# A hybrid attention layer on one core: three engines issue by one written list, values of four heads in one run

## The chip, the cores and the metric
The kernel runs on one NeuronCore of a Trainium2 chip. The core has five engines, each with its own instruction stream: TensorE (PE in the profile, its weight loads PEld), VectorE (DVE), ScalarE (ACT), GpSimd (POOL) and SyncE (SP), which here only issues DMAs. The metric is the device time of one execution in microseconds. Before the change the median of 3 runs is 233.36 us (233.3 to 233.59).

## The reference
One decoder layer for 256 tokens of 1024 channels, fp32, with two attention branches side by side:
```
mod = silu(c) @ w_ada + b_ada;  shift, scale, gate = split(mod, 3)
h = rms_norm(x, g_pre) * (1 + scale) + shift
proj = h @ w_in   # [q_lat 256 | kv_lat 128 | k_rope 32 | z_mla 512 | q,k,v,z_moba 4x512 | merge 2x1024]
# branch A: q = rms_norm(q_lat) @ w_uq, kv = rms_norm(kv_lat) @ w_ukv, rotary part of 32, one shared rotary key
# branch B: 8 heads of 64 with rotary q, k; for 256 tokens its block attention is a causal softmax
y_a = (softmax_A(q k) v * silu(z_mla)) @ w_o_mla;   y_b = (softmax_B(q k) v * silu(z_moba)) @ w_o_moba
y = (sigmoid(merge_a + b) * y_a + sigmoid(merge_b + b) * y_b) @ w_out
out = x + gate * rms_norm(y, g_post)
```

## The kernel before, in words
Precision first: nearly every matrix product of weights is made of three TensorE products of parts. A weight tile is split into a rounded part `w1` (ACT copies it into the type fp32r) and the rest `w2` (VectorE subtracts), and so are the activations (`h1`, `h2`); w1·h1, w1·h2 and w2·h1 are summed in one bank of PSUM. So every weight costs one ACT and one VectorE instruction per 512 columns (`split_one`, L251 to L280), which the profile shows under L266 or, where a helper records the order, under L82. PSUM has eight banks in four names of two each: `acc`, `sc`, `pv`, `tr`.

Weights come by DMA on SP's queue into five buffers `raw` of 8 KB a partition, in the order of `stream` (L200 to L206); `release` (L247) frees one when its last subtraction is issued and `pump` starts the next load. The split parts live in a ring of five tiles (`RING`).

The work has two stages. Up to about 62 us runs the projection of q, k, v of branch B over eight chunks of the contraction, with the modulation of each chunk computed just ahead; its order is written out in strings of tokens (`START`, `STEP`, `LAST`, L44 to L46; `s` is a split, `d` a subtraction, `P` a product, `V` the copy of the values) and kept on the engines by the helper `ordered` (L78). After that follow the latent projection of branch A (`lat_mm`, L516), the rotary embedding of branch B (`moba_rope`, `moba_tr`), 24 groups `F` (L431) that make the SiLU gates (kinds a and b) and the merge gates (kind g) from `win2`, the up-projections (`uq_*`, `ukv_*`), per head the scores and the softmax (`scores`, L656), the transposed probabilities (`p_tr`, L696) and the values of two heads (`pv`, L705), then the output products of both branches (`oproj`, L762), the gate row (`ada_gate`, L728) and the last product with w_out (`out_mm`, L887). A head's softmax is on VectorE mask and maximum (L684, L686), on ACT two exponentials (L689), on VectorE the reciprocal and two products (L690, L693).

In this second stage nothing is ordered by hand. The program issues the pieces in the sequence of L791 to L907, with F and the output products of branch B as fillers, and the framework's planner, which works with its own estimate of durations, places each engine's instructions; so an F may be broken by transposes, scores or values that become ready.

The values of a pair of heads are eight instructions, each head writing its 64 rows of one bank: two passes of 256 columns and two of 128 a head.

Of the kernel before, what the change touches and what calls it, by code (L numbers as in the profile page):

```python
# [18 lines left out]
P = 128  # L19
D = 1024  # L20
S = 256
H = 8
# [23 lines left out]
LAST = "P0v P1v P2v V P0q P0k P1q P2q P1k P2k"  # L46
POOL_LOW = []
# [15 lines left out]
def hybrid_layer_kernel(ctx: ExitStack, tc: tile.TileContext, x, head, cst, gpost, bgate,  # L63
# [128 lines left out]
    def ada_ab(j):  # L192
# [9 lines left out]
    stream += [(("f", 0), win2[0], 2048, 1), (("f", 1), win2[1], 2048, 1), (("uq",), wuq, 1536, 1),  # L202
               (("ukv",), wukv, 1024, 1)]
    stream += [(("f", i), win2[i], 2048, 1) for i in range(2, 12)]
# [17 lines left out]
    for key, src, n, parts in stream:  # L222
        if key[0] != "w":
            loads.append((key, src, 0, n))
        if key == ("out", 0, 0):
            order.append(("gate", 0))
            splits += [(("gate", 0), ("gate",), 0, a, a + 512) for a in (0, 512)]
# [6 lines left out]
        if key[0] == "f" and key[1] >= 8:  # L234
            loads.append((("g", key[1] - 8), wadag[key[1] - 8], 0, 2048))
    held, finished = [0], set()

    def pump():
        while loads and (loads[0] == "m" or held[0] < RAW or loads[0][0] in raws):
# [10 lines left out]

    def split_one():  # L251
        if not splits:
            return False
        u, key, c0, a, b = splits[0]
        if key not in raws or got.get(key, 2048) < c0 + b:
            return False
        if a == 0:
            i = order.index(u)
            if i >= RING and order[i - RING] not in finished:
                return False  # L260
            w1s[u] = rg.tile([P, 1024], FR, name="w1", bufs=RING)
            w2s[u] = rg.tile([P, 1024], FR, name="w2", bufs=RING)
        splits.pop(0)
        r = raws[key][:, c0 + a:c0 + b]
        w = key[0] == "w"
        free = lambda eng, f, *a, **k: f(*a, **k)  # L266
        o = ordered if w else free
        if u == ("w", 0, 0) and a == 0:
            o("V", V.tensor_copy, w1s[u][:, a:b], r)
        else:  # L270
            o("A", act, w1s[u][:, a:b], r, AF.Copy)
        rel = key != ("gate",) and (not splits or splits[0][1] != key)
        if w:
# [28 lines left out]
    def done_with(*us):  # L302
        finished.update(us)
        split_ahead()
# [9 lines left out]
    bR = bank("tr")  # L314

# [75 lines left out]
    def tokens(j, toks):  # L391
        for t in toks.split():
            if t == "s":
                if splits[0][1][0] == "w":
                    assert split_one(), splits[0]
            elif t == "d":
                if subs:
                    sub_one()
# [23 lines left out]
    assert splits[0][1][0] != "w" and not subs and len(vlast) == 2  # L422
    finished.update((("w", KT - 1, 0), ("w", KT - 1, 1)))
    split_ahead()
# [6 lines left out]
    def F():  # L431
        i = fcount[0]
        if i >= 24:
            return
# [9 lines left out]
        done_with(key)  # L444
        kind, m = ORDER[i]
        if kind == "g":
            act(tg[m // 8][:, m % 8], o, AF.Tanh, scale=0.5, bias=bmh[:, m:m + 1])
        else:
            th = wk.tile([P, S], FT, name="th", tag="hf", bufs=2)
            act(th, o, AF.Tanh, scale=0.5)  # L450
            z = wk.tile([P, S], FT, name="sz", bufs=5)
            V.scalar_tensor_tensor(z, th, 1.0, o, op0=OP.add, op1=OP.mult)
            sz[kind, m] = z
# [28 lines left out]
    def moba_tr(w, t):  # L482
        b = bank("tr")
        for i in range(4):
            nc.tensor.transpose(b[:, i * P:(i + 1) * P], rr[w][:, t, i * P:(i + 1) * P], ident)
        src = b.rearrange("p (k n) -> p k n", k=4)
# [15 lines left out]
    qlat = [sb.tile([P, 256], FT, name=f"qlat{t}") for t in range(2)]  # L502
    kvlat = [sb.tile([P, P], FT, name=f"kvlat{t}") for t in range(2)]
    kpe = sb.tile([P, 2, 32], FT, name="kpe")
    qpe = sb.tile([P, 2, 256], FT, name="qpe")
# [10 lines left out]
    def lat_mm():  # L516
        bA.extend(bank("tr") for _ in range(2))
        for i in range(4):
            key = ("l", i // 2, i % 2)
            w1, w2 = (w[:, :2 * NL].rearrange("p (k n) -> p k n", k=2) for w in weights(key))  # L520
            for k in range(2):
                for t in range(2):
                    kk = 2 * i + k
                    o, ha, hb = bA[t][:, :NL], h1[:, kk, t * P:(t + 1) * P], h2[:, kk, t * P:(t + 1) * P]
                    mm(o, ha, w1[:, k], start=(kk == 0), stop=False)
                    mm(o, hb, w1[:, k], start=False, stop=False)
                    mm(o, ha, w2[:, k], start=False, stop=(kk == KT - 1))
            done_with(key)
# [9 lines left out]

    def lat_evac():
        for t in range(2):  # L540
            rope_nat(bA[t][:, 384:416], t, 32, 2, kpe[:, t], V)
# [432 lines left out]
```

## Time and profile before
| | |
|---|---|
| median of 3 runs | 233.36 us |
| the profiled execution: time, span | 233.18 us, 231.4 us |
| TensorE busy, granted clock (mean) | 222.5 us (96%), 0.993 |
| VectorE busy | 169.4 us (73%) |
| ACT busy | 134.3 us (58%) |
| POOL busy | 50.8 us (22%) |
| longest wait of TensorE | 1.0 us |

How to read it: the span runs from the first to the last instruction of the profiled execution, and its time has some overhead around the span. Busy time counts overlapping instructions of one engine once. Matmuls are pipelined: their ends are modelled, so the distance from one start to the next says what one costs. An instruction of VectorE or ACT, too, is shown a little longer than the distance to the next one behind it.

### The profile page before, as it was taken

What the parts mean: (1) busy time and instruction counts of PE and PEld (TensorE: products, weight loads), DVE (VectorE), ACT (ScalarE), POOL (GpSimd) and SP (SyncE); (2) the same over time, 40 slices, a digit from 0 to 9 for tenths busy, and PEclk for the clock granted to TensorE, in tenths of its full rate; (3) what the DMA queues carried; (4) which work ended last, traced back from release to release, by engine and by line L of the source; (5) the groups of instructions that cost most, each with busy time, mean ns of one, the idle gap of its engine ahead of it and who ended that gap; (6) DMA issues with size and microseconds to landing.
All of it is one profiled execution on the core that took longest, in us unless ns stands there. A gap on an engine that the chain in (4) does not pass through costs nothing.

```text
span 231.4 us, 4325 instructions
## 1 busy us (share of the span) xinstructions
PE 222.5 (96%) x1578; PEld 191.6 (83%) x1578; DVE 169.4 (73%) x418; ACT 134.3 (58%) x320; POOL 50.8 (22%) x81
## 2 busy tenths in 40 slices
PE   8989999998999999999999999999999999999990
PEld 8846666665899999989879988989998799988890
DVE  1564554444999668989889998799996566899543
ACT  4364555554956668378775986348676534664320
POOL 2188888100045104300000000000400000562000
PEclk9999999999999999999999999999999999999997
DMA  6999998899855904432520536579799710000022
GB/s 249 348 412 406 378 318 307 274 302 331 314 200 181 353 27 170 129 144 74 187 106 13 173 96 244 208 270 302 290 372 416 292 61 0 1 3 0 0 91 91
DMA packets 10247, 47.05 MB, mean 203 GB/s; under 512 B 1137, under 2 KB 1649, under 8 KB 7154
## 3 DMA queue, kind: packets, MB, share of 16 engines
q1 hardware_dynamic: 10226, 46.78, 55.6%
q8 instruction: 12, 0.20, 0.3%
q14 instruction: 9, 0.07, 0.1%
HBM read 45.73 MB, written 1.05 MB: 202 GB/s over the span
## 4 chain that ended last, share of the span: by engine, by line
PE 91%; DVE 2%; issue 2%; ACT 2%; POOL 0%; POOLq 0%; DVEq 0%; ACTq 0%
PE acc L441 9%; PE acc L443 9%; PE acc L442 9%; PE pv L82 8%; PE sc L82 6%; PE acc L82 6%; PE tr L82 5%; PE pv L710 3%; PE acc L769 3%; PE tr L700 3%; PE acc L770 2%; PE acc L771 2%; PE sc L677 2%; PE sc L669 2%; PE sc L893 2%
## 5 line engine op out<-in xcount | busy, mean ns | idle before, releaser
L266 ACT ACTIVATE w<-raw 128x512 fp32r<-128x512 f32 (+1 forms) x93 | 52.3, 617 | 35.7 <-PE acc L442 9.6
L266 DVE TENSOR_TENSOR w<-raw,w 128x512 fp32r<-128x512 f32 (+1 forms) x93 | 63.8, 726 | 6.8 <-ACT w L266 5.8
L441 PE MATMUL acc<-h,w 128*128 128x256 f32 x184 | 53.1, 289 | 0.1
L443 PE MATMUL acc<-h,w 128*128 128x256 f32 x184 | 52.8, 287 | 0.0
L442 PE MATMUL acc<-h,w 128*128 128x256 f32 x184 | 52.3, 284 | 0.0
L441 PEld LDWEIGHTS acc<-h,w 128*128 128x128 f32 x184 | 34.7, 188 | 1.2 <-issue 0.7
L443 PEld LDWEIGHTS acc<-h,w 128*128 128x128 f32 x184 | 34.7, 188 | 0.6
L442 PEld LDWEIGHTS acc<-h,w 128*128 128x128 f32 x184 | 34.7, 188 | 0.3
L82 DVE TENSOR_TENSOR w<-raw,w 128x512 fp32r<-128x512 f32 x24 | 17.1, 732 | 14.0 <-ACT w L82 13.3
L741 POOL TENSOR_TENSOR gacc<-gacc,bgt 1x1024 f32<-1x1024 f32 x1 | 2.6, 2555 | 68.8 <-DMA raw<-in_wo_dram 68.8
L82 PE MATMUL sc<-w,h 128*128 128x512 f32 x48 | 16.6, 426 | 0.8 <-ACT xnT L82 0.5
L82 PE MATMUL pv<-w,h 128*128 128x512 f32 x48 | 15.5, 407 | 1.0 <-ACT w L82 1.0
L781 POOL TENSOR_TENSOR y<-yy,y 128x256 fp32r<-128x256 f32 x8 | 8.5, 1071 | 36.4 <-ACT y L780 36.4
L82 PE MATMUL acc<-w,h 128*128 128x512 f32 x48 | 15.6, 410 | 0.2 <-ACT h L82 0.2
L82 ACT ACTIVATE w<-raw 128x512 fp32r<-128x512 f32 x23 | 13.7, 619 | 1.6 <-DMA raw<-in_win_dram 1.6
L689 ACT ACTIVATE p<-p,mx 128x128 f32<-128x128 f32 (+1 forms) x32 | 14.2, 447 | 0.3 <-DVE mx L686 0.2
L82 PEld LDWEIGHTS sc<-w,h 128*128 128x128 f32 x48 | 8.0, 189 | 5.2 <-issue 2.9
L82 PEld LDWEIGHTS acc<-w,h 128*128 128x128 f32 x48 | 8.5, 188 | 4.3 <-ACT h L82 2.8
L82 PEld LDWEIGHTS pv<-w,h 128*128 128x128 f32 x48 | 8.5, 188 | 4.3 <-ACT w L82 3.0
L467 POOL TENSOR_TENSOR rr<-rr,m 128x512 f32<-128x512 f32 x4 | 5.6, 1420 | 25.6 <-DVE m L466 25.6
L693 DVE TENSOR_SCALAR p<-p,sm 128x128 f32<-128x128 f32 (+1 forms) x32 | 10.8, 380 | 0.1
L82 ACT ACTIVATE h<-xnT,ab 128x256 fp32r<-128x256 f32 x8 | 4.8, 601 | 10.3 <-DVE ab L82 8.8
(255 smaller groups left out, 525.9 us busy)
## 6 DMA issues: line engine op xcount, KB each, us to landing
raw<-in_win_dram SPq DMA_DIRECT2D x12, 1024.0 KB, 5.0
raw<-in_wada_dram SPq DMA_DIRECT2D x16, 512.0 KB, 7.2
raw<-in_win_dram SPq DMA_DIRECT2D x8, 512.0 KB, 7.6
raw<-in_wadag_dram SPq DMA_DIRECT2D x4, 1024.0 KB, 5.2
raw<-in_wo_dram SPq DMA_DIRECT2D x4, 1024.0 KB, 5.0
raw<-in_wout_dram SPq DMA_DIRECT2D x4, 1024.0 KB, 10.2
raw<-in_win_dram SPq DMA_DIRECT2D x8, 256.0 KB, 7.8
raw<-in_winl_dram SPq DMA_DIRECT2D x2, 832.0 KB, 6.9
```

The costliest lines, as they stand in the source:

```text
L82: r = f(*a, **k)
L266: free = lambda eng, f, *a, **k: f(*a, **k)
L441: mm(o, w1[:, k], h1[:, k], start=(k == 0), stop=False)
L442: mm(o, w1[:, k], h2[:, k], start=False, stop=False)
L443: mm(o, w2[:, k], h1[:, k], start=False, stop=(k == KT - 1))
L467: eng.tensor_tensor(dst, dst, m2, op=OP.add)
L689: act(p[:, a:e], p[:, a:e], AF.Exp, scale=scale, bias=mx[:, t:t + 1], accum_out=sm[:, t:t + 1])
L693: V.tensor_scalar(p[:, a:e], p[:, a:e], sm[:, t:t + 1], None, op0=OP.mult)
L700: nc.tensor.transpose(b[:, i * P:(i + 1) * P], p[:, i * P:(i + 1) * P], ident)
L710: mm(b[64 * i:64 * i + 64, 0:S], v[0][:, h * 64:h * 64 + 64], pTt[br, h][:, 0:S], start=True, stop=False, skip_group_check=True)
L769: mm(o, w1[:, k, c0:c0 + P], u1[br][:, k], start=(k == 0), stop=False)
L781: G.tensor_tensor(y2[:, m], yy, y1[:, m], op=OP.subtract)
```

## The change
TensorE, ACT and VectorE get their instructions in program order (`manual_schedule` for the three), from the first stage to the end; POOL and SP stay with the planner. The second stage is written as a list `PLAN` of 29 lines. A function that yields is a piece in two or three steps: its first token issues TensorE's part, its second (and third) the work on ACT and VectorE. `F` starts a gate group and `f` finishes the oldest one; `sb4` is the scores of heads 4 and 5 of branch b, its second call masks, maxima and exponentials, its third the normalising; `sa3` is one head of branch a; `tb4`, `ta3` transpose, `vb1`, `va0` are values of four heads; `s` and `d` are split and subtraction of the next weight piece, now of 1024 columns (832 for the latent projection); `A`/`y` and `B`/`b` start and finish output products; `G` is one gate sum; `O` the last product. The rest of the edits: values of four heads use one bank and one run; the products with the SiLU gate take 512 columns; loads are held to three from the end of the first stage to the last scores; the rotary key is copied to the other heads by three DMAs instead of two POOL copies and one of VectorE; four small query copies go from VectorE to ACT; the gate bias is added by VectorE.
```diff
-LAST = "P0v P1v P2v V P0q P0k P1q P2q P1k P2k"
+LAST = "s d P0v P1v P2v V s d s d P0q P0k P1q P2q P1k P2k"
...
-            cut = size // 2
-            splits += [(key + (i,), key, c0, a, e) for a, e in ((0, min(cut, m)), (cut, m)) if a < m]
+            cut = 512 if key[0] == "w" else m
+            splits += [(key + (i,), key, c0, a, min(a + cut, m)) for a in range(0, m, cut)]
...
+    in_order = tc.manual_schedule(engines={mybir.EngineType.PE, mybir.EngineType.Activation, mybir.EngineType.DVE})
+    in_order.__enter__()
...
+    cap[0] = RAW - 2
...
-        for x, n, e in ((a0[:, 1], P, "G"), (ak1, S, "V"), (aop["k2"], S, "G")):
-            dict(V=V, G=G)[e].tensor_copy(x[pe, 1:H], x[pe, 0:1].to_broadcast([32, H - 1, n]))
+        for x, n in ((ak1, S), (aop["k2"], S), (a0[:, 1], P)):
+            x = x.bitcast(FT)
+            nc.sync.dma_start(x[pe, 1:H], x[pe, 0:1].to_broadcast([32, H - 1, n]))
...
+    def pv(br, g):
         v = va if br == "a" else vb
         b = bank("pv")
-        for i in range(2):
-            h = 2 * m + i
-            mm(b[64 * i:64 * i + 64, 0:S], v[0][:, h * 64:h * 64 + 64], pTt[br, h][:, 0:S], start=True, stop=False,
+        for n in range(4):
+            h, c0, q = 4 * g + n, S * (n // 2), 64 * (n % 2)
+            mm(b[q:q + 64, c0:c0 + S], v[0][:, h * 64:h * 64 + 64], pTt[br, h][:, 0:S], start=(n < 2), stop=False,
                skip_group_check=True)
...
+        yield
+        u = wk.tile([P, 2, S], FT, name="u", bufs=1)
+        d1, d2 = (x[br][:, 2 * g:2 * g + 2] for x in (u1, u2))
+        V.tensor_tensor(u, b.rearrange("p (k n) -> p k n", k=2), sz[br, g], op=OP.mult)
+        act(d1, u, AF.Copy)
+        V.tensor_tensor(d2, u, d1, op=OP.subtract)
...
+    PLAN = """
+        s d R00 L0 s d R01 L1 s d R10 L2 s d R11 L3 s
+        F ls kr d s
+        F f le d s
+        q00 q01 F f q00 q01 d s
+        lt F f lt d lt s
+        F q10 q11 f d s
+        up F f q10 q11 up d s
+        sb0 un0 un1 F f d sb0 s un0 sb0
+        tb0 tb1 F d s f d tb0 tb1 un1 s
+        un2 un3 F f d un2 s
+        v0 F v1 f un3 d v0 s
+        pe F f v1 pe d s
+        sb2 F f sb2 d s d s
+        sb4 F f sb2 d sb4 s
+        tb2 tb3 sb6 F f sb4 tb2 tb3 d sb6 s
+        tb4 tb5 sa0 F f sb6 tb4 tb5 d sa0 s
+        vb0 sa1 F f sa0 d vb0 sa1 s
+        tb6 tb7 sa2 F f sa1 tb6 tb7 d sa2 s g
+        vb1 ta0 sa3 F f sa2 ta0 d vb1 sa3 s
+        ta1 sa4 F f sa3 ta1 d sa4 s
+        ta2 sa5 F f sa4 ta2 d sa5 s
+        ta3 sa6 F f sa5 ta3 d sa6 s
+        ta4 sa7 F f sa6 ta4 d sa7 s G
+        va0 ta5 F f sa7 ta5 d va0 s G
+        ta6 F f ta6 d s G
+        ta7 B f ta7 d s B b d s va1 B b va1 G B b d s G B b B b d G B b G B b s x
+        A b G A y d s A y A y d s A y A y d s A y A y d s
+        O0 y d s d s O1 gg d s d s O2 O2 d s O3 O3 d s d
+        O4 O4 O5 O5 O6 O6"""
...
+    for tok in PLAN.split():
+        run(tok)
```
The prediction numbers the lines of `PLAN` from 1 ("s d R00 L0 ..."); line 26 begins with `ta7`, line 27 with `A b`, line 28 with `O0`.

## Rows read from the trace of the kernel before
**Rows 1.** The page: busy us, share of the span, instructions of each engine.
```profile
PE 222.5 (96%) x1578; PEld 191.6 (83%) x1578; DVE 169.4 (73%) x418; ACT 134.3 (58%) x320; POOL 50.8 (22%) x81
```
**Rows 2.** Waits of TensorE, longest first: us in total, times, longest.
```profile
PE pv L82 <- ACT w L82: 1.0, 1, 1.0
```
**Rows 3.** Windows: length, busy us of PE, PEld, DVE, ACT, POOL, clock.
```profile
71.02:225.50 154.48, 154.34 (x1167) 140.97 (x1166) 127.09 (x326) 95.67 (x245) 18.56 (x16) 1.00 0.43 156
```
**Rows 4.** TensorE in order of time, an F: start us, us, line, what.
```profile
71.02 0.28 PE L441 MATMUL pv<-h,w 128*128 128x256 f32 x1
71.14 0.28 PE L442 MATMUL pv<-h,w 128*128 128x256 f32 x1
```
**Rows 5.** TensorE in order of time: values of two heads together, F before.
```profile
134.64 0.28 PE L442 MATMUL acc<-h,w 128*128 128x256 f32 x1
134.85 0.65 PE L710 MATMUL pv<-pT,vbt 128*64 128x256 f32 x4
135.33 0.39 PE L714 MATMUL pv<-pT,vbt 128*64 128x128 f32 x4
135.55 0.59 PE L710 MATMUL pv<-pT,vbt 128*64 128x256 f32 x2
```
**Rows 6.** TensorE in order of time: values of two heads in two pieces.
```profile
113.49 0.65 PE L710 MATMUL pv<-pT,vbt 128*64 128x256 f32 x2
114.07 0.38 PE L634 MATMUL pv<-kl,w 128*128 128x256 f32 x1
...
117.16 0.43 PE L710 MATMUL pv<-pT,vbt 128*64 128x256 f32 x1
...
117.96 0.33 PE L624 MATMUL tr<-cstt,qpe 128*128 128x128 f32 x1
```
**Rows 7.** TensorE in order of time: scores of a pair, then one head.
```profile
102.53 0.59 PE L669 MATMUL sc<-m 64*128 64x128 f32 x3
...
103.72 0.39 PE L441 MATMUL acc<-h,w 128*128 128x256 f32 x1
...
115.30 0.49 PE L669 MATMUL sc<-m 64*128 64x128 f32 x2
...
116.08 0.39 PE L442 MATMUL acc<-h,w 128*128 128x256 f32 x1
116.30 0.28 PE L443 MATMUL acc<-h,w 128*128 128x256 f32 x1
```
**Rows 8.** VectorE: groups (count | busy us, mean ns), then in order of time.
```profile
L266 DVE TENSOR_TENSOR w<-raw,w 128x512 fp32r<-128x512 f32 x85 | 59.7, 739 | 6.8 <-ACT w L266 5.8 <-PE acc L443 0.5
L738 DVE SCALAR_TENSOR_TENSOR gacc<-raw,sc,gacc 128x1024 f32<-128x1024 f32 x7 | 8.9, 1279 | 0.0
106.00 1.27 DVE L266 TENSOR_TENSOR w<-raw,w 128x512 fp32r<-128x512 f32 x2
```
**Rows 9.** ACT: 1024 columns as a group, then in order of time.
```profile
L82 ACT ACTIVATE scr<-xs 128x1024 f32<-128x1024 f32 x1 | 1.1, 1058 | 0.4 <-DMA xs<-in_x_dram 0.4
140.05 0.36 ACT L450 ACTIVATE th<-acc 128x256 f32<-128x256 f32 x1
140.32 0.39 ACT L689 ACTIVATE p<-p,mx 128x128 f32<-128x128 f32 x1
141.10 0.19 ACT L689 ACTIVATION_READ_ACCUMULATOR p<-p,mx 128x1 f32 x1
```
**Rows 10.** VectorE in order of time: mask, then a normalising; a group.
```profile
112.96 0.28 DVE L684 CUSTOM_DVE_ANT_0 p<-sc,cstt 128x128 f32<-128x128 f32 x1
113.70 0.55 DVE L693 TENSOR_SCALAR p<-p,sm 128x128 f32<-128x128 f32 x2
L452 DVE SCALAR_TENSOR_TENSOR sz<-th,acc 128x256 f32<-128x256 f32 x8 | 3.3, 412 | 0.0
```
**Rows 11.** The key copy on VectorE; a weight load: KB each, us to landing.
```profile
L571 DVE CAST ak<-ak 32x1792 fp32r<-32x1792 f32 x1 | 2.0, 2000 | 0.0
raw<-in_wo_dram SPq DMA_DIRECT2D x4, 1024.0 KB, 5.0
```

More of the change, by code (lines that the diff above doesn't have):

```diff
@@ L514, in hybrid_layer_kernel, with lat_mm @@
     bA = []
[L516 to L528, printed above, removed]
+    def lat_mm(i):
+        if not bA:
+            bA.extend(bank("tr") for _ in range(2))
+        key = ("l", i // 2, i % 2)
+        w1, w2 = (w[:, :2 * NL].rearrange("p (k n) -> p k n", k=2) for w in weights(key))
+        for k in range(2):
+            for t in range(2):
+                kk = 2 * i + k
+                o, ha, hb = bA[t][:, :NL], h1[:, kk, t * P:(t + 1) * P], h2[:, kk, t * P:(t + 1) * P]
+                mm(o, ha, w1[:, k], start=(kk == 0), stop=False)
+                mm(o, hb, w1[:, k], start=False, stop=False)
+                mm(o, ha, w2[:, k], start=False, stop=(kk == KT - 1))
+        done_with(key)
     def lat_stats():
@@ L549, in lat_tr @@
                 nc.tensor.transpose(b[:, i * S + t * P:i * S + (t + 1) * P], qlat[t][:, i * P:(i + 1) * P], ident)
+        b2 = bank("tr")
+        for t in range(2):
+            nc.tensor.transpose(b2[:, t * P:(t + 1) * P], kvlat[t], ident)
+            nc.tensor.transpose(b2[0:32, S + t * P:S + (t + 1) * P], kpe[:, t], ident)
+        yield
         qlf = wk.tile([P, 2, S], FT, name="qlf", tag="sq", bufs=1)
@@ L602, in uq_pe @@
         done_with(("uq", 1))
+        yield
         for t in range(2):
@@ L773, in oproj @@
             done_with(key)
+        yield
         if br == "b":
@@ L776, in oproj @@
             return
+        if not ys:
+            ys.extend(sb.tile([P, 8, S], FR, name=f"y{i}", tag=f"hy{i}") for i in (1, 2))
         yy = wk.tile([P, S], FT, name="yy", tag="hf", bufs=2)
@@ new lines, in hybrid_layer_kernel, with begin, run @@
+    fq, aq, bq, gens, nxt = [], [], [], {}, dict(A=0, B=0, G=0)
+    makers = dict(up=uq_pe, un0=lambda: uq_nope(0), un1=lambda: uq_nope(1), un2=lambda: ukv_nope(0),
+                  un3=lambda: ukv_nope(1), pe=qpe_tr, lt=lat_tr)
+    plain = dict(s=split_one, d=sub_one, ls=lat_stats, kr=lat_pe, le=lat_evac, g=ada_gate_load, gg=ada_gate_out, x=x_again)
+    def begin(q, g):
+        next(g)
+        q.append(g)
+    def run(tok):
+        c = tok[0]
+        if tok in plain:
+            plain[tok]()
+        elif tok == "F":
+            begin(fq, F())
+        elif tok in ("A", "B"):
+            begin(dict(A=aq, B=bq)[tok], oproj(tok.lower(), nxt[tok]))
+            nxt[tok] += 1
+        elif tok in ("f", "y", "b"):
+            next(dict(f=fq, y=aq, b=bq)[tok].pop(0), None)
+        elif c == "R":
+            moba_rope(int(tok[1]), int(tok[2]))
+        elif c == "L":
+            lat_mm(int(tok[1]))
+        elif c == "G":
+            ada_gate(nxt["G"])
+            nxt["G"] += 1
+        elif tok in gens:
+            next(gens[tok], None)
+        else:
+            if tok in makers:
+                g = makers[tok]()
+            elif c == "q":
+                g = moba_tr(int(tok[1]), int(tok[2]))
+            elif c == "O":
+                g = out_piece(int(tok[1]))
+            elif tok in ("v0", "v1"):
+                g = ukv_v(int(tok[1]))
+            else:
+                g = dict(s=scores, t=p_tr, v=pv)[c](tok[1], int(tok[2]))
+            gens[tok] = g
+            next(g)
+        if tok == "sa7":
+            cap[0] = RAW
+            pump()
```

321 lines of the change are left out of this document (122 added, 199 removed).

## The prediction
> **What bounds the kernel now.** I read the engines' shares first [rows 1]: TensorE is busy 96% of the span at full granted clock, VectorE 73%, ACT 58%. A busy TensorE need not be one at its pace, so next the waits [rows 2]: its longest is 0.99 us, before the last chunk of the first projection. Then one window [rows 3]: from 71.02, where the first gate group F starts, to 225.5, the last matmul, TensorE is busy 154.3 of 154.5 us. Last the spacing of starts, which modelled ends can't blur: a 256-column matmul of F follows the one before by 0.12 us [rows 4], so an F (24 of them) is 2.86 us and 24 F are 68.6. The kernel is bound by TensorE's order and by what one matmul costs in it. VectorE is busy 127 and ACT 96 of those 154 us: both have room on average, the first with little to spare. The profiled execution took 233.18 us (span 231.4 and 1.8 around it), 0.2 below the median of 233.36; sums are made against 233.2.
>
> **The change, part by part.**
> *Values of four heads in one run.* Where two heads' values stand together, eight instructions take 0.70 us (134.85 to 135.55), because the two heads' 64 columns stream side by side: the four passes of 256 columns take 0.48 together (134.85 to 135.33) [rows 5]. Where the planner split them, the same eight take 0.58 + 0.80 = 1.38 us [rows 6]. Of eight such pairs one is together and seven are split: 10.3 us. After: four runs of two pairs, 4 x 1.40 = 5.6. Saved 4.7. A run that breaks into F also costs at its edges: the start before it comes 0.21 instead of 0.12 later [rows 5], the one after 0.22 [rows 7], 0.19 in all; 14 visits become 4: 1.9 saved. Bounds: that only the one pair shows 0.70 allows a saving near 0; all eight at 0.70 is the other end. I take the upper one, as the list leaves nothing to put between, and keep the other as rival 3.
> *Scores of branch b.* A pair kept together takes 1.0 (102.53 to 103.72 less a wait of 0.2), a single head 0.78 [rows 7]; the nine pieces of now sum to 5.6, four pairs to 4.0: 1.6 saved, and five visits fewer, 0.95. TensorE's work so falls by 4.7 + 1.9 + 1.6 + 0.95 = 9.2; no other piece of it changes.
> *1024-column pieces.* VectorE: 512 columns cost 0.60 behind another of the kind (1.27 for two, less the second's end), 256 cost 0.34, so 1024 cost 1.14 by the slope; the nearest 1024-column row, another operation, is 1.28 long, 1.20 in a row [rows 8]. ACT: 1.06 long, 0.96 in a row [rows 9]. Both engines are off TensorE's path now, so this alone moves nothing; it enters below.
> The mean durations (0.739 for 512 columns) say that merging gives back 0.20 a piece. The Trainium skill (VectorE: DVE Perf Modes, section "Mode 2×_2P — use both read ports for one tensor") speaks against it: an fp32 operation on two tensors stays at one result a cycle, so only the fixed part of one instruction goes. By the starts the trace agrees: 0.60 for 512 columns, 1.20 for 1024 of the nearest operation. With 0.20 a piece, twenty pieces in the stretch below would give 2.8 us more than I count, and the sum would be 232.8.
> *Rotary keys by DMA.* This takes 2.0 us from VectorE [rows 11] and two copies from POOL; three small copies stand on SP's queue for about 2 us behind ACT and VectorE, ahead of the next weight load, which has a whole group's time. A load of 1 MB takes 5.0 to land by the same group; the keys are wanted some 40 us later. I cost it at nothing, hidden by those 40 us; without them a score would wait for a landing, 5.0 by that row. The ends are 0 and 5.0, and 0 is the nearer by far.
> *Loads.* Two raw buffers fewer from the end of the first projection until the last scores: the rotary operands hold two of the five in both kernels, and a piece is used up in more than 3.8 us of line, two pieces to a load of 5.0. Nothing; without that cover ACT would wait for a piece, by the 5.0 of a landing at most each time.
> *One list.* The three engines now issue strictly in the order of the 29 lines of the list (counted from "s d R00"). What matters is what returns to ACT and VectorE from each other inside a line. From line 16 on a line goes: ACT's exponentials of a head (0.9 to the next instruction, 0.97 to the last result [rows 9]), then ACT's copy of a weight piece (S, 0.96), then in the next line ACT's tanh of the F before; VectorE there does the SiLU product if that F is of kind a (it needs this tanh), the normalising of the head before, the subtraction D of that same weight piece (needs S), [the three steps of a values run], then mask and maximum of the new head, for which ACT's next exponentials wait. That is a closed ring:
> - plain line: 0.9 + 0.96 + 1.14 + 0.75 (112.96 to 113.70 [rows 10]) and 0.2 for the tails of instructions: 3.9;
> - line with a SiLU product (lines 15, 17, 19, 21): tanh 0.37 [rows 9], the product 0.33 and a normalising 0.55 [rows 10] come in: 0.9 + 0.96 + 0.37 + 0.33 + 0.55 + 1.14 + 0.75 = 5.0;
> - with a values run (17 and 19): 2.0 more for two products of 512 columns at 0.6 with an ACT copy of 0.5 and three tails between: 6.9;
> - line 14 (two D, two heads): 0.96 + 1.14 + 1.1 + 1.14 + 1.5 + 0.97 = 6.9; line 15 with two heads: 6.5.
> TensorE's own lines are 3.85 (14: F 2.86 + a pair 1.0), 4.5, 4.1, 4.95, 4.1, 5.3 and four of 3.77 (F, a head's scores 0.58, which is the 0.78 less its edges, and three transposes 0.33, at most 3 x 0.12); a values run is 1.5 with its edges. Lines 14 to 23: ring 51.7, TensorE 41.9; the ends are no wait at all (the ring covered by banks) and the whole difference of 9.8. TensorE may run ahead only as far as banks go: F of a line needs the bank that the tanh of the line before frees. F of line 23 is so bound to the exponentials of line 21 plus 1.4: 3.8 (line 13 itself: a pair 1.0, two maxima 1.5, the last exponentials 1.0, VectorE 0.3 late) + 43.9 (lines 14 to 21) + 1.4 = 49.1 us from the start of line 13, against 42.8 of TensorE's work: 6.3 waited, first at sb6 in line 15 (its two score banks wait for line 14's maxima), then sa0, vb1 and the F of lines 22 and 23.
> Lines 24 to 27 are VectorE's: ten D (11.4), seven gate sums at 1.2 and the bias row 1.1, two values runs 4.0, eight products of B at 0.34, 2.7, seven pairs of A 4.7, a normalising and tails 1.1: 33.4 us from line 23's exponentials until the second output piece that O0 needs. They start 7.8 after line 21's: 41.2. TensorE goes on from 1.4 after line 21's with three F 8.6, 16 output groups of 12 matmuls 22.5, two values runs 3.0, transposes 1.0 and half of O0 1.4, 36.5 in all: 37.9. It waits 3.3 more.
> In lines 8 and 9 VectorE has un0's evacuation, which waits for ACT's exponentials and a piece, before the normalising that tb0 needs: masks from 2.15 after line 8 begins, exponentials to 4.7, S to 5.65, ACT's copy to 6.0, VectorE's three to 7.1, normalising to 8.15; TensorE is there at 6.6 and has both heads' transposes behind it 1.3 late. Line 13's F and the last subtractions before O2 cost some 0.4 each: 0.7.
> Behind each of these waits everything on TensorE queues: F's weights are ready, but the list holds them behind the waiting instruction. The first 57 us keep their order; the 0.99 us wait stays.
> **Sum:** 233.2 - 9.2 + 6.3 + 3.3 + 1.3 + 0.7 = 235.6.
>
> **Rivals.**
> 1. *TensorE keeps its gain* (faster). If the ring turns faster than I price it, because fewer handoffs lie in it, waits shrink to what banks cover. For it: VectorE and ACT are busy only 82% and 62% of the window [rows 3], and the pieces and key copies take some 5 us more off VectorE. Against: the order, not the load, makes the ring. With a ring of 4.2 on average instead of 5.2 the ten lines lose nothing, lines 24 to 27 lose 2, the rest 2: 233.2 - 9.2 + 4 = 228.0. It decides where ACT's S no longer stands before the tanh that VectorE waits for. Half of that gain lies at 231.
> 2. *The waits eat the gain exactly:* 9.2 of each, 233.2. For it: with D at 1.0, which the mean durations of [rows 8] would allow, the waits of the forecast are 8.8. Against: the starts in the same group.
> 3. *The runs don't pair* (slower). Four heads write one bank, two of them to its second half; if the halves then queue as in the split case, the 4.7 stay unsaved: 240.3. Against: the one contiguous pair did overlap.
>
> **How the numbers follow.** The forecast, waits greater than the gain, 0.46; rival 1 with its halves 0.38; rival 2 0.10; rival 3 and worse 0.06. Within 0.2% (0.5 us, what these runs can tell apart) is rival 2: 0.10; faster 0.38, slower 0.52. The forecast's own range is 234 to 239; with 8 in 10 it reaches down into rival 1, to 228.5, and up to 239.5.
>
> **What would show it.** The matmuls of the values: four runs of about 1.4 us with nothing between, else the gain is wrong. TensorE's list of waits: several us on VectorE and ACT, between 120 and 170 and again before O0, where there were none; VectorE's waits: its SiLU product on ACT's tanh, its D on ACT's S. The window from the first F to the last matmul: 157 us with some 145 of work. If that window is under 150, or TensorE shows under 6 us of idle behind 71, the ring is priced too high and the prediction wrong.

## The result, and the profile after

The changed kernel takes 248.54 us (median of four runs, 248.27 to 248.76) against 233.48 for the kernel before beside it: 1.064 times as long, interval 1.0625 to 1.0662. I had forecast 235.6 and a range of 228.5 to 239.5. The sign is right, the size is not: +15 us instead of +2.4. The profiled execution took 248.5 us, its span is 246.7.

First the page of the profile after: busy time and share of the span for the engines, TensorE and its granted clock in 40 slices, and the chain that ended last.
```profile
span 246.7 us, 4185 instructions
...
PE 222.1 (90%) x1578; PEld 192.3 (78%) x1578; DVE 162.5 (66%) x359; ACT 129.6 (53%) x273; POOL 50.0 (20%) x78
...
PE   8989999998999999799698797989899689979990
...
PEclk9999999999999999799979999999999999999999
...
PE 42%; DVE 30%; ACT 16%; issue 6%; DMA 3%; SPq 1%; POOLq 0%; DVEq 0%; POOL 0%; ACTq 0%
```
The granted clock and the chain on the page of the kernel before:
```profile
PEclk9999999999999999999999999999999999999997
...
PE 91%; DVE 2%; issue 2%; ACT 2%; POOL 0%; POOLq 0%; DVEq 0%; ACTq 0%
```
TensorE fell from 96% [rows 1] to 90% of a longer span, VectorE and ACT do a little less work than before, and almost half of the chain now runs over VectorE and ACT, where it was 4%. No engine got more to do; three engines wait for each other. And the clock line has two dents that the kernel before does not have.

Next the waits of the profile after: those of TensorE, longest first, then three of ACT and VectorE (us in total, times, longest).
```profile
PE acc L771 <- DVE tg L778: 2.6, 2, 1.6
PE acc L424 <- DVE w L81: 2.4, 1, 2.4
PE sc L832 <- DVE w L81: 2.1, 2, 1.7
PE sc L672 <- DVE mx L685: 1.9, 3, 1.2
PE acc L422 <- ACT tg L429: 1.8, 2, 0.9
PE pv L711 <- ACT pT L703: 1.8, 1, 1.8
PE tr L700 <- DVE p L694: 1.7, 1, 1.7
PE pv L81 <- ACT w L81: 1.0, 1, 1.0
...
ACT p L689 <- DVE mx L687: 22.8, 12, 3.2
DVE w L81 <- ACT w L81: 19.1, 18, 2.1
...
DVE sz L435 <- ACT th L432: 10.7, 5, 2.4
```
The wait that was the longest before [rows 2] is now the eighth. The last three lines are the ring of the forecast: ACT's exponentials wait for VectorE's maximum, VectorE's D for ACT's S, the SiLU product for ACT's tanh.

The windows of the profile after (length, then busy us of PE, PEld, DVE, ACT, POOL, clock, DMA share, GB/s): first F to last matmul, then for each of the two dents the stretch ahead of it and its own.
```profile
71.40:240.50 169.10, 153.71 (x1167) 141.50 (x1166) 121.97 (x276) 91.77 (x206) 16.62 (x14) 0.98 0.40 143
100.00:102.00 2.00, 0.98 (x5) 0.54 (x6) 1.79 (x8) 1.69 (x4) 0.00 (x0) 1.00 0.00 0
102.00:106.00 4.00, 4.00 (x23) 4.00 (x23) 3.25 (x5) 2.30 (x7) 0.00 (x0) 0.57 0.45 143
120.00:123.00 3.00, 0.58 (x6) 0.32 (x3) 2.53 (x5) 1.91 (x3) 0.00 (x0) 0.96 0.00 0
123.00:126.00 3.00, 3.00 (x14) 3.00 (x15) 2.59 (x11) 1.04 (x5) 0.00 (x0) 0.50 0.58 191
```
The window is 169.1 us long, where it was 154.5 [rows 3] and I had forecast 157. That is 14.6 of the 15.3 us by which the span grew. TensorE's 153.7 busy us are not 153.7 us of work at full pace: between 102 and 106 and between 123 and 126 the granted clock is 0.57 and 0.50, mostly and wholly the lower of its two levels (1.2 GHz), each time behind a stretch in which TensorE had been busy for half of the time or less.

I summed the distances from each matmul's start to the next over this window, and took what one lasts beyond its usual distance as a wait where that is 0.25 us or more. Work: values 5.8 us where they were 10.2, scores 8.2 (10.8), F at full clock 70.1 (72.5), but transposes 5.6 (4.2): 8.0 us saved. (These are taken from e11 below, which has the same matmuls in nearly the same order and hardly a wait.) Waits: 18.3 us. Lower clock: 0.213 instead of 0.12 us a matmul, 2.9 us in all (1.5 behind 102 and 1.4 behind 123, against the same matmuls in the execution of e1 below, which kept the full clock there). Distances that are longer by less than 0.25 us make up the rest: -8.0 + 18.3 + 2.9 + 1.4 = 14.6. The 157 us with 145 of work that I forecast are 169 with 146.

### The profile page after: what moved, and what is told of

Read it like the earlier page. It is cut to its first block, busy times and chain, and to the rows that moved or that the text cites. A ratio compares the mean times of both kernels' runs of the same rounds, so it can differ in the third digit from the quotient of the medians.

```text
span 246.7 us, 4185 instructions
## 1 busy us (share of the span) xinstructions
PE 222.1 (90%) x1578; PEld 192.3 (78%) x1578; DVE 162.5 (66%) x359; ACT 129.6 (53%) x273; POOL 50.0 (20%) x78
## 4 chain that ended last, share of the span: by engine, by line
PE 42%; DVE 30%; ACT 16%; issue 6%; DMA 3%; SPq 1%; POOLq 0%; DVEq 0%; POOL 0%; ACTq 0%
DVE w L81 13%; ACT p L689 6%; ACT w L81 6%; PE sc L81 5%; PE acc L81 5%; PE pv L81 5%; PE tr L81 4%; DMA raw<-in_wada_dram 3%; DVE p L685 3%; PE acc L424 2%; PE acc L423 2%; PE acc L422 2%; DVE gacc L739 2%; DVE p L694 2%; PE sc L832 1%
## 5 line engine op out<-in xcount | busy, mean ns | idle before, releaser
L81 DVE TENSOR_TENSOR w<-raw,w 128x1024 fp32r<-128x1024 f32 (+2 forms) x71 | 74.4, 1062 | 19.8 <-ACT w L81 19.1
L81 ACT ACTIVATE w<-raw 128x1024 fp32r<-128x1024 f32 (+2 forms) x70 | 61.1, 894 | 4.8 <-PE tr L510 3.0
L422 PE MATMUL acc<-h,w 128*128 128x256 f32 x184 | 54.4, 296 | 2.2 <-ACT tg L429 1.8
L424 PE MATMUL acc<-h,w 128*128 128x256 f32 x184 | 53.4, 290 | 2.4 <-DVE w L81 2.4
L423 PE MATMUL acc<-h,w 128*128 128x256 f32 x184 | 53.1, 288 | 0.0
L422 PEld LDWEIGHTS acc<-h,w 128*128 128x128 f32 x184 | 36.1, 196 | 3.4 <-ACT tg L429 2.2
L424 PEld LDWEIGHTS acc<-h,w 128*128 128x128 f32 x184 | 36.1, 196 | 2.6 <-DVE w L81 2.6
L423 PEld LDWEIGHTS acc<-h,w 128*128 128x128 f32 x184 | 36.2, 197 | 0.0
L786 POOL TENSOR_TENSOR y<-yy,y 128x256 fp32r<-128x256 f32 x8 | 10.0, 1265 | 116.4 <-ACT y L785 116.4
L81 PE MATMUL pv<-w,h 128*128 128x512 f32 x48 | 15.3, 407 | 1.0 <-ACT w L81 1.0
L449 POOL TENSOR_TENSOR rr<-rr,m 128x512 f32<-128x512 f32 x4 | 7.8, 1954 | 24.6 <-DVE m L448 24.5
L771 PE MATMUL acc<-u1b,w 128*128 128x256 f32 x32 | 9.6, 299 | 2.7 <-DVE tg L778 2.6
L785 ACT ACTIVATE y<-yy 128x256 fp32r<-128x256 f32 x8 | 3.3, 418 | 15.8 <-DVE yy L784 15.8
L435 DVE SCALAR_TENSOR_TENSOR sz<-th,acc 128x256 f32<-128x256 f32 x8 | 3.4, 421 | 10.8 <-ACT th L432 10.7
L81 ACT ACTIVATE rws<-tr 128x256 f32<-128x256 f32 x8 | 3.1, 384 | 13.7 <-PE tr L81 13.7
L81 ACT ACTIVATE h<-xnT,ab 128x256 fp32r<-128x256 f32 x8 | 4.8, 601 | 10.2 <-DVE ab L81 8.8
```

The source lines that it names most:

```text
L81: r = f(*a, **k)
L422: mm(o, w1[:, k], h1[:, k], start=(k == 0), stop=False)
L423: mm(o, w1[:, k], h2[:, k], start=False, stop=False)
L424: mm(o, w2[:, k], h1[:, k], start=False, stop=(k == KT - 1))
L435: V.scalar_tensor_tensor(sz[kind, m // 2][:, m % 2], th, 1.0, o, op0=OP.add, op1=OP.mult)
L449: eng.tensor_tensor(dst, dst, m2, op=OP.add)
```

## The experiments

Two theories. Theory 1 is that of the forecast: the fixed order, not the load, makes ACT and VectorE late, because steps that nobody waits for stand ahead of steps that TensorE waits for. Theory 2: pieces of 1024 columns and VectorE's sum of work make them late in any order. All ratios are to the kernel before.

**e1: masks ahead of D in lines 13 to 23.** Where a line has a values run, its steps come last. The edit, on a plain line (the others alike):
```diff
-        ta1 sa4 F f sa3 ta1 d sa4 s
+        ta1 sa4 F f sa3 ta1 sa4 d s
```
Line 13 of the changed kernel reads `sb2 F f d sb2 s d s`; in the list printed with the change its first `d` stands behind the second `sb2`, which is the order that e1 gives it.

> The changed kernel with one thing different in lines 13 to 24 of the list: VectorE's mask and maximum of the new heads (and so ACT's exponentials) come ahead of the subtraction D of that line instead of behind it, and where the line has a values run its three steps come last. Nothing else, the same instructions. Theory 1 (the order makes the ring: D stands ahead of the mask that ACT's exponentials wait for, and ACT's copy S ahead of the tanh): the ring of a plain line loses D's 1.14, from about 4.05 to 2.9, less than TensorE's 3.8, so most of the 7.3 us that TensorE waits between 130 and 175 goes: 241 to 243 us. The waits ahead of 130 (1.8, 0.7, 2.9) and behind 185 (some 5.6) stay. Theory 2 (VectorE and ACT have too much work and too long pieces, whatever the order): within 1 us of 248.5.

Measured 238.59 us, 1.0234 (1.0201 to 1.0266): 9.9 us less than the changed kernel, with the same instructions. The waits of lines 15 to 23 went but for 0.3 at sa0. Theory 2 is out for this stretch. It gave more than I expected, and the clock tells most of why. The windows of e1 over the two places where the changed kernel lost its clock:
```profile
101.00:105.00 4.00, 3.96 (x30) 3.52 (x31) 3.88 (x8) 1.99 (x7) 0.00 (x0) 1.00 0.21 41
120.00:123.00 3.00, 0.58 (x5) 0.33 (x3) 2.50 (x5) 1.91 (x3) 0.00 (x0) 1.00 0.00 0
123.00:127.00 4.00, 4.00 (x35) 3.73 (x36) 2.93 (x12) 3.17 (x10) 0.00 (x0) 1.00 0.75 260
```
The wait is the same (0.58 us busy of three in both kernels), yet the clock stayed full in this execution. So the same wait costs 1.4 us more or nothing: from the matmul that ends it to the next scores TensorE takes 4.2 us in the changed kernel and 2.8 in e1. The runs of e1 point the same way: 237.97 and 238.38 us at a mean clock of 0.996, 238.79 at 0.983, 239.79 at 0.972. As TensorE comes earlier to lines 10 and 11, it waits 1.4 us more there (un3, v1): 7.0 of the masks' waits, 2.9 of clock and 1.2 of the B groups less 1.4 are 9.7 of the 10.5 us by which the span of the profiled execution is shorter; the rest lies in distances that differ by less than 0.25 us.

**e2: no fixed order.** The list gives the sequence in which the program is written, the planner places all engines.
```diff
-    in_order.__enter__()
...
-    in_order.__exit__(None, None, None)
```


> The changed kernel without the fixed order: the list only gives the order in which the instructions are written, and the planner places them on TensorE, ACT and VectorE as it does in the kernel before. Four-head values, pieces of 1024 columns and keys by DMA stay. Theory 1 (the waits come from the fixed order): TensorE's waits fall from 18 to under 5 and the time comes to 228 to 234, with the clock at its upper level. Theory 2 (long pieces and load): still 240 or more. If the planner splits the four-head runs again, some of the 6.9 us of saved work is lost as well.

229.93 us, 0.9889 (0.9826 to 0.9952). All other edits together gain 3.5 us by the medians (1.1 to 4.1 by the interval), and the fixed order of the list costs 18.6. In its window one wait of 1.1 us is left, and the planner again breaks values into F (11 visits, 8.1 us).

**e3, e4, e12: single edits in the kernel before.** Values of four heads in one run (e3), pieces of 1024 columns (e4), rotary keys by DMA (e12), in this order in the diff.
```diff
-        for i in range(2):
-            h = 2 * m + i
-            mm(b[64 * i:64 * i + 64, 0:S], v[0][:, h * 64:h * 64 + 64], pTt[br, h][:, 0:S], start=True, stop=False,
+        for n in range(4):
+            h, c0, q = 4 * g + n, S * (n // 2), 64 * (n % 2)
+            mm(b[q:q + 64, c0:c0 + S], v[0][:, h * 64:h * 64 + 64], pTt[br, h][:, 0:S], start=(n < 2), stop=False,
...
-            cut = size // 2
+            cut = size // 2 if key[0] == "w" else size
...
-            dict(V=V, G=G)[e].tensor_copy(x[pe, 1:H], x[pe, 0:1].to_broadcast([32, H - 1, n]))
+            nc.sync.dma_start(x[pe, 1:H], x[pe, 0:1].to_broadcast([32, H - 1, n]))
```


> The kernel before, with the values of four heads in one run (one bank, one product, one copy, one subtraction for two pairs; the SiLU products of two heads' pairs kept in one buffer) and nothing else of the change. The trace of the changed kernel has four such runs of 1.25 us of starts each where the kernel before has 10.2 us for all values. Theory 1: the gain is real by itself, and where the planner keeps a run together it gives up to 4 us: 229 to 231. Rival: the planner breaks the runs up again, or a longer evacuation makes TensorE wait: 233 to 235.

232.23 us, 0.9952 (0.9935 to 0.9970): 1.1 us, as the planner breaks the runs into 11 visits and 8.5 us. The gain is there; only an order that keeps the run together collects the other 2.7.

> The kernel before, with the weight pieces behind the first projection copied and subtracted in 1024 columns (832 for the latent) instead of 512 (416), nothing else of the change. Theory 1: alone this moves nothing, 232.5 to 234.5, as the planner puts masks and evacuations between the pieces. Theory 2 (the long pieces are what makes TensorE wait, in any order): 237 or more.

232.84 us, 0.9973 (0.9960 to 0.9986): 0.6 us faster. Long pieces cost nothing where something may be put ahead of them. This and e2 end theory 2's first half; the list itself was not run with pieces of 512 columns.

> The kernel before, with the rotary keys of seven heads copied by three DMAs on SP's queue instead of one copy on VectorE and two on POOL; nothing else. Theory 1 (the keys are wanted some 40 us later, and the weight loads behind the three DMAs have room): 232.5 to 234, no difference, or 0.5 less for the 2 us off VectorE. Rival (SP's queue stands behind ACT and VectorE and holds the weight loads): 235 or more.

231.69 us, 0.9905 (0.9873 to 0.9936): 1.8 us faster, which I had not expected from an engine off the path. VectorE is busy 167.4 us instead of 169.4. TensorE had no wait to lose; the planner now breaks F into 36 visits instead of 40 and scores into 15 instead of 18, and by the distances of starts F, scores and values cost 2.6 us less. Why the planner places them so I did not test. 1.1 + 0.6 + 1.8 = 3.5 is the gain of e2 by the medians. That may be chance: e2's interval is wide, and it holds the other edits and the new sequence too.

**e7: the list binds TensorE alone.**
```diff
-    in_order = tc.manual_schedule(engines={mybir.EngineType.PE, mybir.EngineType.Activation, mybir.EngineType.DVE})
+    in_order = tc.manual_schedule(engines={mybir.EngineType.PE})
```


> The changed kernel, with the list binding for TensorE alone: ACT and VectorE are placed by the planner, everything else stays. It asks whose order it is that costs. Theory 1 (TensorE's order is good, the waits come from the order of ACT and VectorE): 226 to 231, below the planner's 229.9 if the planner puts masks and evacuations early. Rival (TensorE's strict order by itself costs, because one late operand holds all that is behind): 236 or more.

237.19 us, 1.0157 (1.0120 to 1.0193), the rival's side. Its waits of TensorE:
```profile
PE tr L467 <- POOL rsl L521: 2.3, 1, 2.3
PE tr L700 <- DVE raw L573: 2.2, 1, 2.2
PE pv L641 <- DVE raw L579: 1.3, 1, 1.3
```
So 7.3 us come already when TensorE alone must follow the list, and the planner, which may put the steps of the others elsewhere, delays what TensorE is held for. Binding ACT and VectorE as well costs 11.3 more, 18.6 in all. These are differences of times and not parts of the same waits: the first row is no wait of the changed kernel. I had put it all on ACT and VectorE.

**e5: lines 8 to 12 as well.** Masks ahead of D there too, D of line 12 ahead of `pe`, each bank's evacuation as one run of ACT and then one run of VectorE, and two of the four rotary query copies on ACT. The main part of the diff, against e1:
```diff
-        sb0 un0 un1 F f d sb0 s un0 sb0
-        tb0 tb1 F d s f d tb0 tb1 un1 s
-        un2 un3 F f d un2 s
-        v0 F v1 f un3 d v0 s
-        pe F f v1 pe d s
+        sb0 un0 un1 F f sb0 d sb0 un0 s
+        tb0 tb1 F un1 d s f tb0 tb1 d s
+        un2 un3 F un2 f d s
+        v0 F v1 un3 f v0 d s
+        pe F f d v1 pe s
...
-        V.tensor_copy(a0[p, 1, hs], src[:, :, 0:P])
-        act(ak1[p, hs], src, AF.Copy)
-        V.tensor_tensor(aop["k2"][p, hs], src, ak1[p, hs], op=OP.subtract)
+        for (p, hs), src in pairs:
+            act(ak1[p, hs], src, AF.Copy)
+        for (p, hs), src in pairs:
+            V.tensor_tensor(aop["k2"][p, hs], src, ak1[p, hs], op=OP.subtract)
+            V.tensor_copy(a0[p, 1, hs], src[:, :, 0:P])
```


> The kernel with the masks ahead of D (238.6 us), and besides in lines 8 to 12 the same idea: masks ahead of D, the evacuation of a projection's bank as one run of ACT's copies and then one run of VectorE's steps (before: ACT and VectorE in turn, up to eight handoffs in a bank), un1's evacuation ahead of the weight piece, and D ahead of the rotary queries' evacuation. The copies of two of the four rotary query blocks move from VectorE to ACT; the instructions are otherwise the same. Theory 1 (the handoffs in the fixed order make the waits at tb0, at un3, at v1 and at the F of line 13): these four, 1.8, 0.5, 1.7 and 2.6 in the trace of that kernel, go: 232 to 233.5. Theory 2 (load): VectorE is as late with any order, 237 or more.

231.28 us, 0.9897 (0.9864 to 0.9931): 7.3 us less than e1, and the waits at tb0, un3, v1 and the F of line 13 are gone. It changes the order and the evacuations at once; which of the two each wait needed was not run. For the longest, of 2.6 us at the F of line 13, the trace of e5 tells, with the D that F needs and the first and last step of `pe`:
```profile
111.25 1.22 DVE L81 TENSOR_TENSOR w<-raw,w 128x1024 fp32r<-128x1024 f32 x1
...
112.39 0.37 ACT L567 ACTIVATE raw<-tr 32x256 fp32r<-32x256 f32 x1
...
116.47 0.42 DVE L573 TENSOR_TENSOR raw<-tr,raw 32x256 fp32r<-32x256 f32 x1
```
`pe` still takes 4.5 us (5.2 in the changed kernel), but D no longer stands behind it. So there the order was enough, without the grouped evacuation.

**e9: e5's lines 8 to 12 in the changed kernel.** The diff of e5, without that of e1; of it, line 12:
```diff
-        pe F f v1 pe d s
+        pe F f d v1 pe s
```

> The changed kernel with the new lines 8 to 12 alone; lines 13 to 24 keep D ahead of the mask. Theory 1: the waits of lines 9 to 13 go (1.8, 0.7, 2.9), and the stretches at the lower clock with them (0.21 us a matmul instead of 0.12 in the two F behind these waits, 3.6 us in all), while the waits of 130 to 175 stay: 239 to 240.5, and with the masks' own gain the two parts add up. Rival (the clock falls behind the waits that stay as well): 241 to 244.

242.05 us, 1.0361 (1.0329 to 1.0393). 6.5 us less than the changed kernel, where e1 gave 9.9 and both together 17.3: nearly additive. But the clock fell all the same, later, as the rival said. (In the changed kernel the lower clock had cost 2.9 us, not the 3.6 that I counted.) The windows of e9:
```profile
122.00:126.00 4.00, 2.62 (x16) 1.63 (x14) 3.90 (x16) 0.79 (x3) 0.00 (x0) 0.99 0.61 203
126.00:130.00 4.00, 3.76 (x20) 3.47 (x20) 1.54 (x8) 3.57 (x12) 0.00 (x0) 0.50 0.16 65
```
Behind 122 to 126, where the waits of sb6 leave TensorE 2.6 us busy of four, it runs at the lower level.

**e6: e5, and the end of the list.** Two gate sums earlier, the bias row on POOL, `b` ahead of gate sums, gate weights loaded two loads earlier.
```diff
-        ta1 sa4 F f sa3 ta1 sa4 d s
+        ta1 sa4 F f sa3 ta1 sa4 d s G
...
-            V.tensor_tensor(a[0:1], a[0:1], gt["b"], op=OP.add)
+            G.tensor_tensor(a[0:1], a[0:1], gt["b"], op=OP.add)
...
+    G_AFTER = [("f", 10), ("f", 11), ("ob", 0), ("ob", 1)]
```


> The kernel of the run with the new lines 8 to 12, and besides at the end: two gate sums move from lines 26 and 27 to lines 20 and 22, the bias row goes to POOL, the evacuations b stand ahead of the gate sums, and the loads of the gate weights come two loads earlier. Theory 1: the waits of 0.9 and 1.2 in the B groups and of 1.8 and 0.6 in O0 and O1 go as well, 227.5 to 230, as in lines 20 and 22 VectorE has 1.3 us free. Theory 2 (VectorE's sum of work from line 20 on is what binds): the waits move to another place, 231 to 234.

234.19 us, 1.0033 (1.0007 to 1.0060), 2.9 us worse than e5. ACT's waits between 150 and 205:
```profile
ACT w L81 <- DMA raw<-in_wo_dram: 7.2, 3, 2.8
```
The early gate weights push the output weights back (their first load is issued at 160.0 us, in e5 at 147.7), ACT's S stands waiting for them, the tanh queues behind S, and TensorE waits 2.0 us for the tanh. VectorE's earlier sums bought nothing against that.

**e8: e5, and the end in another way. e10: the same without the fixed order**, by the diff of e2.
```diff
-        sb2 F f sb2 d s d s
+        sb2 F f s sb2 d d s
...
-        ta7 B f ta7 d s B b d s va1 B b va1 G B b d s G B b B b d G B b G B b s x
+        ta7 B f ta7 d s G B b d s va1 B b B b va1 d s B b G B b d G B b G B b s x
...
+        G.memset(a, 0.0)
+        G.tensor_copy(a[0:1], gt["b"])
```


> The kernel with masks ahead of D and the new lines 8 to 12 (231.3 us), with three more steps. In line 13 ACT's first S stands ahead of the exponentials, so that the second D need not wait for an S behind them (in that trace VectorE idles 1.0 us there, and sb6 in line 15 then waits 1.1 and sa0 0.3). In line 26 the evacuations b stand ahead of a values run and of the gate sums, and one gate sum fills the time in which VectorE waited for the first B. The bias row is the start of the gate's accumulator, written by POOL in line 20, and VectorE's 1.2 us for it go. The loads keep their order, as the moved loads made ACT wait 7.2 us for landings in the run before. Theory 1: waits of 1.4, some 1.5 of the 2.0 in the B groups and 0.8 of the 2.4 in O0 and O1 go: 227.5 to 229. Theory 2 (VectorE's work from line 24 on binds): the B waits come back in front of O0, 229.5 to 231.

229.94 us, 0.9840 (0.9807 to 0.9874). The waits of lines 15 and 16 went but for 0.3; those of the B groups did not (2.4 us). The time falls into the range of theory 2, but for another reason: VectorE itself waited there for TensorE, as the row of its waits between 170 and 190 shows:
```profile
DVE tg L777 <- PE acc L772: 2.3, 2, 2.1
```


> The best list so far (the run with the new end) with the fixed order taken away: the planner places TensorE, ACT and VectorE, from the instructions as this list writes them. It asks whether a good list still costs against the planner. Theory 1 (a fixed order costs only what its handoffs add): the planner breaks values and scores into F again, 228.5 to 230.5, not below the list. Rival: the planner fills what waits are left, under 228.

229.66 us, 0.9831 (0.9803 to 0.9859): the planner neither beats this list nor loses to it. It has no wait in the window, but 10 visits of values and 8.0 us for them.

**e11: e8, with lines 26 to 28 written again.**
```diff
-        ta7 B f ta7 d s G B b d s va1 B b B b va1 d s B b G B b d G B b G B b s x
-        A b G A y d s A y A y d s A y A y d s A y A y d s
-        O0 y d s d s O1 gg d s d s O2 O2 d s O3 O3 d s d
+        ta7 B f ta7 d s G B b d s va1 B b d s B b va1 B b G B b d B b G B b G s x
+        A b G A y d s A y d s A y d s A y d s A A y A y
+        O0 y y d s d s O1 gg d s d s O2 O2 d s O3 O3 d s d
```


> The list of the run with the new end (229.9 us), with lines 26 to 28 written once more: the third subtraction of line 26 goes into the 2.1 us in which VectorE waited for the third B, and in line 27 each subtraction stands one product earlier, so that the two weight pieces of O0 come ahead of the last four products, which only O2 needs. Theory 2 of the run before (VectorE's sum of work from line 24 on binds): only the 2.1 us that VectorE idled can be won, as its other work up to the pieces of O2 is the same: 227.5 to 228.5. Rival (the order in front of O0 is no limit any more, the pieces wait for the ring): 229.5 or more.

226.79 us, 0.9705 (0.9680 to 0.9729): faster than both kernels, 6.7 us under the one before and 21.7 under the changed one, and better than I expected. Its window from the first F to the last matmul, and the only wait of TensorE in its list that lies in this window:
```profile
71.20:218.42 147.22, 146.53 (x1166) 137.83 (x1166) 118.60 (x273) 92.84 (x208) 17.53 (x16) 1.00 0.45 164
```
```profile
PE sc L831 <- DVE w L81: 0.6, 1, 0.6
```
TensorE is busy 146.5 of 147.2 us and bound by its own work again. That is past rival 1, whose 228.0 still held 4 us of waits. It was reached by another order and by moving a few steps off VectorE (the bias row to POOL, two query copies to ACT). How much of the 6.7 us is the order's is open: under the planner e8's list has 229.66 us (e10), and this last list was not run under it.

## Why the prediction was right in sign and wrong in size

The mechanism was for the most part the forecast one: a fixed order in which steps that nobody waits for stand ahead on ACT and VectorE. Two steps of the forecast failed. It put the rotary queries' evacuation in line 12 at nothing, and with it lines 10 to 13 at 0.4; they waited 3.6 us. And it counted every matmul at the full clock; that cost 2.9 us. Of the 12.9 us between 235.6 and 248.5 these are 6.1. The rest are terms that were sized too small: 1.7 up to O0, 1.4 of short waits, 1.2 of work, 1.0 in lines 14 to 23, 0.5 in lines 8 and 9, 0.3 in line 28, and 0.7 outside the window.

*The work saved, 9.2 forecast.* 8.0 measured. A values run of four heads in the changed kernel (in order of time: start, us, line, what, count):
```profile
142.48 1.08 PE L711 MATMUL pv<-pT,vbt 128*64 128x256 f32 x8
143.40 0.61 PE L715 MATMUL pv<-pT,vbt 128*64 128x128 f32 x8
143.93 0.38 PE L672 MATMUL sc<-a 96*128 96x128 f32 x1
```
From 142.48 to 143.93 it is 1.45 us; I had 1.40. So the halves of a bank pair as [rows 5] let hope and rival 3 is out; rival 2 too, as the waits are twice the gain. Scores came as counted (2.6 us). Missing is 1.2: transposes now stand alone in front of a group and cost 1.4 more, which I had not counted.

*Lines 14 to 23, 6.3 forecast.* 7.3 measured, at the places named: sb6 1.0, sa0 1.4, vb1 2.1, the F of lines 21 to 23 1.1, 0.6 and 1.1 (I had those of 22 and 23). From mask to mask the lines take 4.05, 4.05, 4.04 and 4.04 plain (forecast 3.9), 5.3 with a SiLU product (5.0), 7.4 and 7.3 with a values run (6.9). One turn of the ring, from the trace of the changed kernel in order of time:
```profile
163.63 1.04 ACT L81 ACTIVATE w<-raw 128x1024 fp32r<-128x1024 f32 x1
...
164.57 0.45 ACT L429 ACTIVATE tg<-acc,bmh 128x256 f32<-128x256 f32 x1
164.70 1.23 DVE L81 TENSOR_TENSOR w<-raw,w 128x1024 fp32r<-128x1024 f32 x1 [0.20 <-ACT w L81]
...
165.08 0.38 PE L422 MATMUL acc<-h,w 128*128 128x256 f32 x1 [0.92 <-ACT tg L429]
165.84 0.28 DVE L685 CUSTOM_DVE_ANT_0 p<-sc,cstt 128x128 f32<-128x128 f32 x1
...
166.78 0.40 ACT L689 ACTIVATE p<-p,mx 128x128 f32<-128x128 f32 x1 [1.38 <-DVE mx L687]
```
S ends, D starts; D ends, the mask starts; the mask ends, the exponentials start; the tanh that F waits for has to stand behind all of it. D is as priced: the two D in the next fence take 2.36 together, 1.14 and the second's full 1.22. The term is right to 1 us. (Two sums of the ring are rounded loosely, line 14's terms give 6.8 and a plain line's 3.95; that moves nothing.) Which link decides I had wrong in rival 1: I said S ahead of the tanh. e1 left S there and moved only D and the values steps behind the mask, and nearly every wait of these lines went.

That 7.3 came so near to 6.3 is in part luck. The sum ran from the start of line 13, which I had priced in the order printed with the change, with the masks first. From there (119.28) to the last exponentials of the line it takes 7.5 us and not 3.8, as VectorE is 2.3 us later than I had it and then does a D of 1.2 first. Lines 14 to 21 take 46.3 and not 43.9, so F of line 23 comes after 55.1 instead of 49.1. But TensorE was late as well: it had lost 2.6 us of wait and 1.4 of clock in line 13 itself, which hid 4.0 us of the ring.

*Lines 8 and 9, 1.3 forecast:* 1.8, at tb0 as said.

*Lines 10 to 13, 0.4 forecast:* this step failed. I priced the rotary queries' evacuation (`pe`, line 12) at nothing and gave line 13's F 0.4. Measured are 0.7 at v1 and 2.9 at that F (2.6 in one wait and 0.3 right behind it). VectorE and ACT in order of time, from the trace of the changed kernel; in brackets the idle time ahead and what ended it:
```profile
116.51 0.42 DVE L569 COPY a<-tr 32x256 f32<-32x256 f32 x1 [0.26 <-PE tr L620]
...
116.96 0.37 ACT L572 ACTIVATE raw<-tr 32x256 fp32r<-32x256 f32 x1
...
117.37 0.42 DVE L573 TENSOR_TENSOR raw<-tr,raw 32x256 fp32r<-32x256 f32 x1 [0.44 <-ACT raw L572]
...
117.80 0.42 DVE L569 COPY a<-tr 32x256 f32<-32x256 f32 x1
...
118.25 0.37 ACT L572 ACTIVATE raw<-tr 32x256 fp32r<-32x256 f32 x1 [0.91 <-DVE a L569]
...
121.70 2.36 DVE L81 TENSOR_TENSOR w<-raw,w 128x1024 fp32r<-128x1024 f32 x2
...
122.98 0.58 PE L424 MATMUL acc<-h,w 128*128 128x256 f32 x1 [2.42 <-DVE w L81]
```
Four blocks, each with VectorE's copy, then ACT's, then VectorE's subtraction, take turns for 5.2 us (116.51 to 121.70); behind them stands the D whose weights F needs. ACT's copy does not read what VectorE's copy writes, yet starts only when that has ended: both read the same part of one bank. The Trainium skill (PSUM — Partial Sum Buffer, section "PSUM bank collisions raise a hardware error ⚠️") says that the compiler back end's scheduler adds a dependency between two engines on the same bank and the same 32 partitions, two reads included; that ACT idled 0.91 us until VectorE's copy had ended agrees. In the kernel before the same chain takes 15.4 us (118.65 to 134.05), because the planner put masks, D and exponentials between its links; nobody waited for it. In e5 D stands ahead of the chain, and the wait at the F of line 13 went.

*Lower clock, not forecast:* 2.9 us. The F at 102 and the one at 123 run in the stretches with a granted clock of 0.57 and 0.50 shown above. TensorE in order of time behind the wait at tb0:
```profile
103.03 0.41 PE L423 MATMUL acc<-h,w 128*128 128x256 f32 x1
103.24 0.41 PE L424 MATMUL acc<-h,w 128*128 128x256 f32 x1
...
105.87 0.28 PE L422 MATMUL acc<-h,w 128*128 128x256 f32 x1
105.99 0.28 PE L423 MATMUL acc<-h,w 128*128 128x256 f32 x1
```
The starts are 0.21 apart, then 0.12 as in [rows 4]. I had taken the full clock of [rows 3] for granted, in a kernel that I forecast to wait.

*Lines 24 to 27, 3.3 forecast:* 5.0 measured, 3.2 in the B groups and 1.8 in front of O0's second piece. The forecast had one sum for both. What it lacks comes from a price. I counted D at 1.14 beside POOL's `y`; POOL and VectorE in order of time:
```profile
208.93 2.53 POOL L786 TENSOR_TENSOR y<-yy,y 128x256 fp32r<-128x256 f32 x2 [0.81 <-ACT y L785]
209.11 1.76 DVE L81 TENSOR_TENSOR w<-raw,w 128x1024 fp32r<-128x1024 f32 x1
```
A D here lasts 1.76 instead of 1.22, three times, 1.6 us, nearly all of the 1.7. The Trainium skill (SBUF — State Buffer, section "🔬 SBUF: two separate sides") says that VectorE with two SBUF inputs and a GpSimd instruction that reads SBUF take turns at a shared port pair, each for a whole instruction; the 0.54 us and the second of the two products on POOL, which takes 1.7 where others take 0.85, agree. Line 28 waited 0.6 more.

*Keys by DMA, 1024-column pieces and fewer raw buffers, at nothing.* Keys and pieces gain under the planner, 1.8 (e12) and 0.6 (e4). In the list none of the three made TensorE wait: it has no wait for a key or a landing behind the first projection.

*The sum with what was measured:* 233.2 - 8.0 + 1.8 + 3.6 + 7.3 + 5.0 + 0.6 (all waits, 18.3) + 2.9 (clock) + 1.4 (short waits) + 0.7 (the first F 0.4 later, and the tail) = 248.5.

## What to carry to other kernels

A list that binds several engines is as good as its worst handoff: walk along it, ask of each step on ACT and VectorE who waits for it, and put those that TensorE waits for first. An evacuation that changes engine can run as one stretch of each; alone, that was not run here. Check also what looks free, loads and evacuations included, by what stands behind it in its queue. And where a forecast holds long waits of TensorE, its range needs room for the lower clock behind them.

## What the runs showed of the hardware that I had not expected

The clock did not fall behind the same wait every time: the windows at 120 to 123 and what follows are at 0.50 in the changed kernel and at 1.00 in e1, with equal busy time in the window ahead (0.58 of 3 us). Within one kernel (e1) this spreads the runs by 1.8 us, 237.97 to 239.79, in step with the mean clock from 0.996 to 0.972. So a difference below 2 us between two kernels that both wait need not be their order; e5, e8 and e11, which wait less, spread by 1.0, 0.4 and 0.5 us. The clock is not the only cause of spread: e2, with one wait of 1.1 us, has a run of 232.51 beside three of 229.44 to 230.15, at a mean clock of 0.989 beside 0.992 to 0.994; what made it longer is open.
